# Modulation products of a decoder step on one Trainium2 core: 256 or 512 columns per product

## The chip, the core and the metric

The kernel runs on one core of a Trainium2 chip. The metric is device time in microseconds (us) of one execution; the median of three runs of the kernel before is 2639.03 us (2635.15 to 2641.7). In the profile PE is TensorE's matmul stream, PEld its weight loads, DVE is VectorE, ACT is ScalarE, POOL is GpSimd and SP is SyncE, which issues nearly all DMAs.

## The reference

One step of a decoder layer for 256 prompt tokens and 8 x 4 sample tokens (288 in all), width 4096, all in fp32. The part that matters here is the modulation of the normalised input, and of the output, by a projection of nine condition vectors (one prompt, eight samples):

```
m = jax.nn.silu(c) @ w_ada + b_ada                 # c: 9 x 4096, w_ada: 4096 x 12288
shift, scale, gate = jnp.split(m[:, None, :], 3, axis=-1)
h = _rmsnorm(x, g_norm) * (1 + scale) + shift
... = _split_in(h @ w_in)                          # w_in: 4096 x 14960, feeds three token mixers
x = x + gate * (mix @ w_out)                       # w_out: 4096 x 4096
```

The three mixers (a chunked gating MLP, a gated delta rule, a sparse attention with cached keys) lie between and are not touched.

## The kernel before

A planner in the kernel (class `Weaver`) holds a list of units and writes out every engine's instructions, running a model of the engines' times as it goes. A `Gemm` unit (kind "g") multiplies one 128-row k-tile of `w_in` or `w_out` by `h`: the raw weight tile is split by ACT and DVE into a high and a low part (`wh`, `wl`), and PE does three products for each of four 128-column tiles (`acc<-hH,wh`, `hL,wh`, `hH,wl`, 288 columns each). Raw tiles hold two k-tiles (512 KB) and rotate through `N_RAW` = 4 buffers `w`; splits run up to `N_SPLIT` = 4 units ahead of PE.

An `Ada` unit (kind "a") is a piece of `silu(c) @ w_ada`. Its stationary operand is 32 columns of `cT`, its moving operand a weight tile, and four products go to the four column quadrants of the array (`tile_position=(0, 32 * q)`), each into its own 32 partitions of one PSUM bank `ada`. Before, a unit loads one 512 KB tile and each quadrant takes 256 columns. Shift and scale are made in 11 sets, the first six of two k-tiles of `h` each and then five of four (`STEPS`, `ada_first`, tiles `wa`, `N_ADA` = 4 buffers), and gate in 4 sets (`ada_gate`, which uses the four `w` buffers). A set adds up over all of `w_ada`'s rows: 16 or 32 units. When it is complete, ACT copies the bank to SBUF, PE transposes it (`ada<-ident,adasb`), DVE adds the bias (`ada_raw`, `ada_fin1`, `ada_fin2`), and for shift and scale `make_h` makes the next rows of `h`.

Two stages follow each other. In the first (to about 812 us) the units of the next sets are spread between `Gemm` units of 45 column tiles per step; `LEAD` says how many units beyond a set's end are to be done when its step begins. In the second stage a gate unit follows every `GATE` = 4 `Gemm` units until all 128 are done (about 825 to 2062 us); the mixers' work is woven in between. Then come the output projection's units alone.

The list is kept in order on every queue: `prefetch` loads units strictly one after another as buffers come free (a unit whose buffer is taken holds up the loads of all units behind it), and SP issues the DMAs in that order. PE executes `Ada` units where they stand in the list.

Of the kernel before, what the change touches and what calls it, by code (L numbers as in the profile page):

```python
# [19 lines left out]
P = 128  # L20
# [29 lines left out]
GPAIR = 1  # L50
PLAN = {"p1": ["zc0", "zc1", "zb0", "zb1", "zb2", "zb3"], "attn": ["za0", "za1"], "dn3": []}
# [36 lines left out]
class Weaver:  # L88
# [214 lines left out]
    def prefetch(self, cur):  # L303

        u = self.units
        go = True
        while go:
            go = False
            if self.split < self.loaded:
                x = u[self.split]  # L310
                if x.kind == "a":
                    self.split += 1
                    go = True
                elif self.n_split < N_SPLIT and (self.at(x.raw.w) <= self.t["T"] + 0.5 or
                                                 not any(y.kind == "g" for y in u[cur + 1:self.split])):
# [20 lines left out]
    def run(self):  # L336
        self.prefetch(-1)
        for i, x in enumerate(self.units):
            for f in x.pre:
                f()  # L340
            self.finish(x.need)
            while self.split <= i:
                self.prefetch(i - 1)
            for n in range(x.steps):
                x.mm(n)
                if n == x.steps - 1:
                    if x.kind == "a":
                        self.release(x.tag, self.t["T"])
                    else:
                        self.n_split -= 2 if x.with_ else 1  # L350
                self.prefetch(i if n == x.steps - 1 else i - 1)
                self.stages()
            for f in x.post:
                f()
        self.finish(list(self.gens))


class Unit:
    def __init__(self, kind, tag, steps):
        self.kind, self.tag, self.steps = kind, tag, steps  # L360
        self.pre, self.need, self.post = [], [], []
        self.loads = True


class Box:
# [9 lines left out]
def tile_hybrid_step(ctx: ExitStack, tc: tile.TileContext, I, O):  # L375
# [134 lines left out]
    class Ada(Unit):  # L510
# [5 lines left out]
        def __init__(self, st, segs, ks, nk, finish, tag):  # L516
            super().__init__("a", tag, 1)
            self.st, self.segs, self.ks, self.nk, self.finish = st, segs, ks, nk, finish

        def do_load(self):  # L520
            n = sum(s[1] for s in self.segs)
            if self.tag == "wa":
                self.w = tl("p1", [P, self.nk, n], "wa", N_ADA)
            else:
                self.w = W.tile(wpool, [P, self.nk, n], F32, "w", "w", N_RAW)
            rows = w_ada[self.ks * P:(self.ks + self.nk) * P]
            if len(self.segs) == 2:
                (c0, m), (c1, _) = self.segs
                for k in range(self.nk):
                    dma(self.w[:, k].rearrange("p (s c) -> p s c", s=2),  # L530
                        rows[k * P:(k + 1) * P].rearrange("p (s c) -> p s c", c=c1 - c0)[:, 0:2, c0:c0 + m])
            else:
                ((c0, m),) = self.segs
                dma(self.w, rows[:, c0:c0 + m].rearrange("(k p) c -> p k c", p=P))

        def mm(self, j):
            if self.ks == 0:
                W.take()
                self.st.ps = pr("ada")
            n = sum(s[1] for s in self.segs) * self.nk // 4  # L540
            for q in range(4):
                k, o = (q % 2, q // 2) if self.nk == 2 else (0, q)
                kk = self.ks + k
                T.matmul(self.st.ps[32 * q:32 * q + 32, 0:n], cT[:, 9 * kk:9 * kk + 32], self.w[:, k, o * n:(o + 1) * n],
                         start=self.ks == 0, stop=self.ks + self.nk == KT, tile_position=(0, 32 * q))
            if self.ks + self.nk == KT:
                W.push(self.finish, front=True)

    def ada_raw(st, n):
        sb = W.tile(tmp, [P, 256], F32, "adasb", "adasb", 1)  # L550
        A.copy(sb[:, 0:n], st.ps[:, 0:n])
        yield
        free()
        yield from bank()
        p2 = pr4("ada2")
        for c in range(n // P):
            T.transpose(p2[:, c], sb[:, c * P:(c + 1) * P], ident)
        st.p2 = p2
        yield

    def ada_fin1(st, k0, n):

        yield from ada_raw(st, 256)
        yield lambda: prep_gens[0].done
        for which in range(2):
            src = st.p2[:, 0:2].rearrange("p h (q r) -> p q h r", r=32)[:, 2 * which:2 * which + 2, :, 0:9]
            dst = mod[which][:, k0:k0 + n, :].rearrange("p (q h) r -> p q h r", h=2)
            b = bT[:, which * 32 + k0:which * 32 + k0 + n].rearrange("p (q h) -> p q h", h=2)
            if n == 2:
                V.tensor_tensor(dst[:, 0], src[:, 0], b[:, 0, :, None].to_broadcast([P, 2, 9]), op=OP.add)  # L570
                V.tensor_tensor(dst[:, 0], dst[:, 0], src[:, 1], op=OP.add)
            else:
                V.tensor_tensor(dst, src, b[:, :, :, None].to_broadcast([P, 2, 2, 9]), op=OP.add)
            if which == 1:
                dst = mod[which][:, k0:k0 + n, :]
# [5 lines left out]
        yield from make_h(k0, n)  # L581

    def ada_fin2(st, f):
        yield from ada_raw(st, 256)
        src = st.p2[:, 0:2].rearrange("p h (q r) -> p q h r", r=32)[:, :, :, 0:9]
        b = bT[:, 64 + 8 * f:64 + 8 * f + 8].rearrange("p (q h) -> p q h", h=2)
        dst = gtT[:, 8 * f:8 * f + 8, :].rearrange("p (q h) r -> p q h r", h=2)
        V.tensor_tensor(dst, src, b[:, :, :, None].to_broadcast([P, 4, 2, 9]), op=OP.add)
# [1876 lines left out]
```

## Time and profile before

| | |
|---|---|
| median of three runs | 2639.03 us |
| the profiled execution | 2654.27 us, span 2652.5 us, mean granted PE clock 0.986 |
| busy: PE / PEld / DVE / ACT / POOL | 97% / 86% / 61% / 40% / 19% |
| DMA over the span | 616.11 MB, 232 GB/s |

Times of the trace come from that one execution; us count from its first instruction. "acc", "ada", "wa" are tile names; all instructions have line L71, since a recording layer issues them. One `ada` product shows as two records on PE, each with its weight load, so "x8" in a row of the timeline is one unit of four products. A record's length includes the time until its result is out, so what a run of instructions takes from PE is read from the starts of the instructions around it.

### The profile page before, as it was taken

How to read it: one execution, taken by the hardware profiler on the slowest of the kernel's cores; microseconds unless marked ns; L12 is line 12 of the kernel's file. 1: busy time of each engine (PE TensorE's matmuls, PEld its weight loads, DVE VectorE, ACT ScalarE, POOL GpSimd, SP SyncE). 2: the span in 40 equal slices, each digit the busy share in tenths (PEclk: the TensorE clock that was granted, in tenths of full speed). 3: DMA queues.
4: the chain of work that ended last, by engine and by line, in shares of the span. 5: the costliest groups of instructions: out<-in, count | busy, mean ns of one | idle time of the engine just before them, and what ended most of it. 6: DMA issues, size and time to landing. Idle time of an engine off the chain costs nothing.

```text
span 2652.5 us, 55324 instructions
## 1 busy us (share of the span) xinstructions
PE 2560.9 (97%) x21190; PEld 2279.1 (86%) x21190; DVE 1623.5 (61%) x3611; ACT 1062.0 (40%) x2440; POOL 492.3 (19%) x1137
## 2 busy tenths in 40 slices
PE   6999999999999999999999999999999999999997
PEld 3788888888888888877789989989989989999997
DVE  3477665555568786744467576567566567555554
ACT  3423222222245343333344444444443544444443
POOL 2000000000001042153543333343340210000000
PEclk9999999999999999999999999999999999999998
DMA  8999998998757576686776676577568565555565
GB/s 289 345 320 321 342 315 296 304 312 307 232 153 217 178 238 217 200 283 221 266 233 192 182 242 207 177 241 233 179 195 261 149 202 181 178 182 175 177 186 164
DMA packets 376032, 616.11 MB, mean 232 GB/s; under 512 B 48840, under 2 KB 149436, under 8 KB 375768
## 3 DMA queue, kind: packets, MB, share of 16 engines
q1 hardware_dynamic: 364728, 574.66, 67.8%
q0 software_dynamic: 11040, 37.92, 4.3%
q8 instruction: 167, 2.74, 0.4%
q14 instruction: 97, 0.79, 0.1%
HBM read 587.54 MB, written 24.95 MB: 231 GB/s over the span
## 4 chain that ended last, share of the span: by engine, by line
PE 86%; DMA 6%; DVE 2%; issue 2%; POOL 2%; ACT 1%; SPq 0%; another core or an unknown queue 0%; ACTq 0%; POOLq 0%; DVEq 0%
PE acc L71 68%; PE ada L71 7%; DMA wa<-in_w_ada_dram 2%; PE kT L71 1%; PE Sup L71 1%; DMA kraw<-in_cache_k_dram,ixk 1%; DVE wl L71 1%; PE YP L71 1%; DMA w<-in_w_in_dram 1%; PE v L71 1%; PE gram L71 1%; DMA vraw<-in_cache_v_dram,ixv 1%; PE o L71 1%; POOL vraw L71 1%; PE S L71 0%
## 5 line engine op out<-in xcount | busy, mean ns | idle before, releaser
L71 DVE TENSOR_TENSOR wl<-w,wh 128x512 fp32r<-128x512 f32 (+1 forms) x1216 | 806.1, 682 | 735.3 <-ACT wh L71 667.8
L71 ACT CAST wh<-w 128x512 fp32r<-128x512 f32 (+1 forms) x1216 | 717.3, 611 | 1232.3 <-PE acc L71 905.6
L71 PE MATMUL acc<-hH,wh 128*128 128x288 f32 (+1 forms) x3744 | 1180.2, 315 | 14.5 <-ACT hH L71 7.4
L71 PE MATMUL acc<-hL,wh 128*128 128x288 f32 (+1 forms) x3744 | 1110.4, 297 | 0.6 <-DVE hL L71 0.4
L71 PE MATMUL acc<-hH,wl 128*128 128x288 f32 (+1 forms) x3744 | 1108.4, 296 | 2.6 <-DVE wl L71 1.8
L71 PEld LDWEIGHTS acc<-hH,wh 128*128 128x128 f32 (+1 forms) x3744 | 708.4, 189 | 152.0 <-issue 81.9
L71 PEld LDWEIGHTS acc<-hL,wh 128*128 128x128 f32 (+1 forms) x3744 | 710.1, 190 | 6.7 <-issue 5.5
L71 PEld LDWEIGHTS acc<-hH,wl 128*128 128x128 f32 (+1 forms) x3744 | 709.1, 189 | 4.0 <-DVE wl L71 3.6
L71 PE MATMUL acc<-mL,wh 128*128 128x288 f32 x1024 | 302.6, 295 | 2.6 <-DVE mL L71 2.6
L71 PE MATMUL acc<-mH,wh 128*128 128x288 f32 x1024 | 304.4, 297 | 0.0
L71 PE MATMUL acc<-mH,wl 128*128 128x288 f32 x1024 | 302.7, 296 | 0.0
L71 PEld LDWEIGHTS acc<-mL,wh 128*128 128x128 f32 x1024 | 193.0, 189 | 2.9 <-DVE mL L71 2.9
L71 PEld LDWEIGHTS acc<-mH,wh 128*128 128x128 f32 x1024 | 193.0, 188 | 0.2
L71 PEld LDWEIGHTS acc<-mH,wl 128*128 128x128 f32 x1024 | 193.0, 188 | 0.0
L71 PE MATMUL ada<-wa,cT 128*32 128x256 f32 x2048 | 159.2, 395 | 15.8 <-DMA wa<-in_w_ada_dram 14.3
L71 PEld LDWEIGHTS ada<-wa,cT 128*32 128x32 f32 x2048 | 50.2, 109 | 66.9 <-issue 39.8
L71 DVE TENSOR_TENSOR zb<-zb,acc 128x288 f32<-128x288 f32 x160 | 70.9, 452 | 47.0 <-PE acc L71 45.7
L71 POOL TENSOR_TENSOR htmp<-yT,gaT 128x32 f32<-128x32 f32 x20 | 7.7, 382 | 460.0 <-DVE gaT L71 460.0
L71 PE MATMUL ada<-w,cT 128*32 128x256 f32 x1024 | 83.9, 393 | 1.9 <-issue 1.0
L71 POOL TENSOR_SCALAR frs<-frs 128x1 f32<-128x1 f32 (+1 forms) x3 | 0.9, 298 | 451.5 <-DVE frs L71 451.3
L71 DVE TENSOR_TENSOR R<-R,R 128x248 f32<-128x248 f32 (+30 forms) x248 | 72.6, 293 | 7.1 <-DMA R<-dD 0.5
L71 POOL TENSOR_SCALAR tap<-xp,cwT 128x32 f32<-128x32 f32 x144 | 75.8, 527 | 0.3
(457 smaller groups left out, 2387.0 us busy)
## 6 DMA issues: line engine op xcount, KB each, us to landing
w<-in_w_in_dram SPq DMA_DIRECT2D x464, 512.0 KB
wa<-in_w_ada_dram SPq DMA_DIRECT2D x160, 512.0 KB
w<-in_w_ada_dram SPq DMA_DIRECT2D x128, 512.0 KB
w<-in_w_out_dram SPq DMA_DIRECT2D x128, 512.0 KB
wa<-in_w_ada_dram SPq DMA_DIRECT2D x192, 256.0 KB
St<-in_state_dn_dram SPq DMA_DIRECT2D x16, 512.0 KB
out_dram<-St SPq DMA_DIRECT2D x16, 512.0 KB
X<-in_x_prompt_dram SPq DMA_DIRECT2D x8, 512.0 KB
```

The lines of the kernel that those rows point to most:

```text
L71: r = f(*a, **k)
```

## The change

A unit now takes two weight tiles (`n_load` = 2, `do_load` runs twice and appends to `w`). Each quadrant multiplies 512 columns: quadrants 0 and 1 take the two halves of the first tile, 2 and 3 those of the second. For shift and scale sets of two k-tiles the four quadrants are four different k-tiles; for the others each pair of quadrants is one k-tile. So there are half as many units of twice the width, and at the end of a set the quadrants hold partial sums that DVE adds. Per set the copy is 512 columns wide instead of 256 (from a tag `u2k` of two buffers that the conv stage's `prev` and `tailo` use too), and there are four transposes instead of two. `LEAD` goes from 10 to 5 and `GATE` from 4 to 8 units, the same number of tiles. Bytes, number and size of the DMAs stay.

```
-LEAD = 10
+LEAD = 5
-GATE = 4
+GATE = 8
...
                     x.do_load()
-                    self.loaded += 1
+                    x.n_load -= 1
+                    if not x.n_load:
+                        self.loaded += 1
...
                     if x.kind == "a":
-                        self.release(x.tag, self.t["T"])
+                        for _ in x.w:
+                            self.release(x.tag, self.t["T"])
...
         def mm(self, j):
...
-            n = sum(s[1] for s in self.segs) * self.nk // 4
             for q in range(4):
-                k, o = (q % 2, q // 2) if self.nk == 2 else (0, q)
-                kk = self.ks + k
-                T.matmul(self.st.ps[32 * q:32 * q + 32, 0:n], cT[:, 9 * kk:9 * kk + 32], self.w[:, k, o * n:(o + 1) * n],
+                kk = self.ks + q * self.nk // 4
+                w = self.w[q // 2].rearrange("p k n -> p (k n)")[:, q % 2 * 512:q % 2 * 512 + 512]
+                T.matmul(self.st.ps[32 * q:32 * q + 32], cT[:, 9 * kk:9 * kk + 32], w,
                          start=self.ks == 0, stop=self.ks + self.nk == KT, tile_position=(0, 32 * q))
...
-    def ada_raw(st, n):
-        sb = W.tile(tmp, [P, 256], F32, "adasb", "adasb", 1)
-        A.copy(sb[:, 0:n], st.ps[:, 0:n])
+    def ada_raw(st):
+        sb = W.tile(tmp, [P, 512], F32, "u2k", "adasb", 2)
+        A.copy(sb, st.ps)
...
-        for c in range(n // P):
+        for c in range(4):
             T.transpose(p2[:, c], sb[:, c * P:(c + 1) * P], ident)
...
             if n == 2:
-                V.tensor_tensor(dst[:, 0], src[:, 0], b[:, 0, :, None].to_broadcast([P, 2, 9]), op=OP.add)
-                V.tensor_tensor(dst[:, 0], dst[:, 0], src[:, 1], op=OP.add)
+                V.tensor_reduce(dst, st.p2[:, :, 2 * which:2 * which + 2].rearrange("p q c r -> p c r q"),
+                                axis=AX.X, op=OP.add)
+                V.tensor_tensor(dst, dst, b, op=OP.add)
             else:
-                V.tensor_tensor(dst, src, b[:, :, :, None].to_broadcast([P, 2, 2, 9]), op=OP.add)
+                V.tensor_tensor(dst, st.p2[:, which], b, op=OP.add)
+                V.tensor_tensor(dst, dst, st.p2[:, 2 + which], op=OP.add)
...
-        nk = 4 // n
+        nk = 8 // n
...
-        return [Ada(st, [(2 * D + f * 1024, 1024)], k, 1, fin, "w") for k in range(KT)]
+        return [Ada(st, [(2 * D + f * 1024, 1024)], k, 2, fin, "w") for k in range(0, KT, 2)]
```

Where the units stand is the planner's to say, so the order of the instructions is shown at three places. First PE, in the first step of the first stage, between two column tiles of `acc`; before:

```order
L71 MATMUL acc_1400<-hH_530,wh 128x288
L71 MATMUL acc_1400<-hL_542,wh 128x288
L71 MATMUL acc_1400<-hH_530,wl 128x288
L71 MATMUL ada<-wa,cT 32x256 x4
L71 MATMUL acc_1417<-hH_530,wh 128x288
L71 MATMUL acc_1417<-hL_542,wh 128x288
```

and now:

```order
L71 MATMUL acc_1413<-hH_500,wh 128x288
L71 MATMUL acc_1413<-hL_512,wh 128x288
L71 MATMUL acc_1413<-hH_500,wl 128x288
L71 MATMUL ada<-wa,cT 32x512 x4
L71 MATMUL acc_1447<-hH_500,wh 128x288
L71 MATMUL acc_1447<-hL_512,wh 128x288
```

"x4" is one unit, with 256 and with 512 columns. Before, PE's order has 102 such single units in the first stage and 75 runs of two or more in a row (256 units in 177 runs); now 128 units stand in 125 runs. Behind the first `acc` product the runs go from 166 to 119: from 72 to 60 in the six steps of two k-tiles, and from 94 to 59 after them. In the second stage, where every gate unit stands alone, they go from 128 to 64.

Second, SP's queue in the second stage, where `w<-in_w_ada_dram` is a gate tile and `w<-in_w_in_dram` a raw tile of a `Gemm` pair; before:

```order
L71 DMA w<-in_w_in_dram 128x2x512
L71 DMA mixD_185<-pz 128x256
L71 DMA w<-in_w_in_dram 128x2x512
L71 DMA w<-in_w_ada_dram 128x1024
L71 DMA w<-in_w_in_dram 128x2x512 x2
L71 DMA w<-in_w_ada_dram 128x1024
```

and now:

```order
L71 DMA prev<-in_state_conv_dram 24x512
L71 DMA w<-in_w_in_dram 128x2x512 x4
L71 DMA w<-in_w_ada_dram 128x1024 x2
L71 DMA w<-in_w_in_dram 128x2x512 x4
L71 DMA w<-in_w_ada_dram 128x1024 x2
```

Two raw tiles and one gate tile by turns became four raw tiles and two gate tiles, which share the same four buffers.

Third, DVE at the end of a shift and scale set of four k-tiles (`shT`, `gaT` are the shift and the scale, `zc` a running sum of the step); before:

```order
L71 TENSOR_TENSOR zc_918<-zc_918,acc_4138 128x288
L71 TENSOR_TENSOR shT<-ada_4119,bT 128x36
L71 TENSOR_TENSOR gaT<-ada_4119,bT 128x36
L71 SCALAR_TENSOR_TENSOR gaT<-gaT,gnT 128x36
L71 TENSOR_TENSOR zc_935<-zc_935,acc_4149 128x288
```

and now:

```order
L71 TENSOR_TENSOR zc_879<-zc_879,acc_3897 128x288
L71 TENSOR_TENSOR shT<-ada_3876,bT 128x36
L71 TENSOR_TENSOR shT<-shT,ada_3876 128x36
L71 TENSOR_TENSOR gaT<-ada_3876,bT 128x36
L71 TENSOR_TENSOR gaT<-gaT,ada_3876 128x36
L71 SCALAR_TENSOR_TENSOR gaT<-gaT,gnT 128x36
```

Each of the two rows of the modulation got one more add, of the other pair of quadrants.

## Rows read from the trace of the kernel before

**Rows 1.** The page, part 4: the chain that ended last, by engine.
```profile
PE 86%; DMA 6%; DVE 2%; issue 2%; POOL 2%; ACT 1%; SPq 0%; another core or an unknown queue 0%; ACTq 0%; POOLq 0%; DVEq 0%
```

**Rows 2.** Windows: us, busy PE, PEld, DVE, ACT, POOL, PEclk, DMA share, GB/s.
```profile
55.00:358.00 303.00, 300.07 (x2600) 245.60 (x2600) 191.15 (x420) 103.38 (x207) 14.64 (x48) 0.99 0.97 322
358.00:735.00 377.00, 371.89 (x3116) 311.93 (x3112) 205.20 (x409) 109.94 (x203) 10.87 (x32) 1.00 0.87 292
812.00:1050.00 238.00, 220.90 (x2123) 190.21 (x2122) 179.84 (x471) 100.00 (x256) 53.35 (x114) 0.96 0.67 209
1050.00:1500.00 450.00, 434.84 (x3622) 377.13 (x3622) 259.15 (x554) 183.87 (x468) 184.98 (x373) 0.98 0.71 228
1500.00:2060.00 560.00, 557.68 (x4610) 503.95 (x4609) 375.46 (x956) 251.48 (x695) 186.00 (x471) 1.00 0.70 215
```

**Rows 3.** Timeline of PE, one unit alone: start us, us, instruction.
```profile
265.79 0.29 PE L71 MATMUL acc<-hH,wl 128*128 128x288 f32 x1
266.01 0.64 PE L71 MATMUL ada<-wa,cT 128*32 128x256 f32 x8
266.58 0.40 PE L71 MATMUL acc<-hH,wh 128*128 128x288 f32 x1
266.82 0.29 PE L71 MATMUL acc<-hL,wh 128*128 128x288 f32 x1
266.95 0.29 PE L71 MATMUL acc<-hH,wl 128*128 128x288 f32 x1
```

**Rows 4.** Timeline of PE, two modulation units in a row.
```profile
118.67 0.29 PE L71 MATMUL acc<-hH,wl 128*128 128x288 f32 x1
118.89 1.07 PE L71 MATMUL ada<-wa,cT 128*32 128x256 f32 x16
119.89 0.40 PE L71 MATMUL acc<-hH,wh 128*128 128x288 f32 x1
120.13 0.29 PE L71 MATMUL acc<-hL,wh 128*128 128x288 f32 x1
```

**Rows 5.** Timeline of PE, one gate unit in the second stage.
```profile
1506.34 0.29 PE L71 MATMUL acc<-hH,wl 128*128 128x288 f32 x1
1506.57 0.64 PE L71 MATMUL ada<-w,cT 128*32 128x256 f32 x8
1507.13 0.40 PE L71 MATMUL acc<-hH,wh 128*128 128x288 f32 x1
1507.37 0.29 PE L71 MATMUL acc<-hL,wh 128*128 128x288 f32 x1
```

**Rows 6.** Tiles ada and Sup: duration ns min/median/max, first and last start, forms.
```profile
L71 PE MATMUL ada<-wa,cT x2048: 379/379/637, 20.1 to 730.4; 128*32 128x256 f32 x187
L71 PE MATMUL Sup<-R,R x64: 590/592/697, 1521.7 to 2165.4; 128*128 128x512 f32 x64
```

**Rows 7.** Timeline of PE, the transposes that end a modulation set.
```profile
1171.81 0.30 PE L71 MATMUL acc<-hH,wl 128*128 128x288 f32 x1
1171.94 0.38 PE L71 MATMUL ada<-ident,adasb 128*128 128x128 f32 x2
...
1172.29 0.29 PE L71 MATMUL acc<-hL,wh 128*128 128x288 f32 x1
```

**Rows 8.** Tile ada, and groups of ACT by shape: copies of two widths.
```profile
L71 ACT COPY adasb<-ada x15: 363/373/434, 50.3 to 2065.2; 128x256 f32<-128x256 f32 x15
L71 ACT COPY ktk<-kT 128x512 f32<-128x512 f32 x32 | 18.8, 588 | 28.3 <-PE kT L71 11.5 <-issue 8.5 <-ACT S L71 8.2
```

**Rows 9.** Waits of PE, PEld (55 to 741 us), ACT (812 to 2180).
```profile
PE acc L71 <- ACT hH L71: 7.4, 2, 4.0
PE ada L71 <- DMA wa<-in_w_ada_dram: 2.0, 2, 1.5
PEld ada L71 <- DMA wa<-in_w_ada_dram: 7.4, 15, 2.0
ACT wh L71 <- DMA w<-in_w_in_dram: 84.5, 36, 4.1
```

More of the change, by code (lines that the diff above doesn't have):

```diff
@@ L361, in __init__ @@
         self.pre, self.need, self.post = [], [], []
-        self.loads = True
+        self.loads, self.n_load = True, 1
 class Box:
@@ L518, in __init__ @@
             self.st, self.segs, self.ks, self.nk, self.finish = st, segs, ks, nk, finish
+            self.n_load, self.w = 2, []
         def do_load(self):
             n = sum(s[1] for s in self.segs)
+            nk = self.nk // 2
             if self.tag == "wa":
-                self.w = tl("p1", [P, self.nk, n], "wa", N_ADA)
+                w = tl("p1", [P, nk, n], "wa", N_ADA)
             else:
-                self.w = W.tile(wpool, [P, self.nk, n], F32, "w", "w", N_RAW)
-            rows = w_ada[self.ks * P:(self.ks + self.nk) * P]
+                w = W.tile(wpool, [P, nk, n], F32, "w", "w", N_RAW)
+            ks = self.ks + nk * len(self.w)
+            rows = w_ada[ks * P:(ks + nk) * P]
             if len(self.segs) == 2:
                 (c0, m), (c1, _) = self.segs
-                for k in range(self.nk):
-                    dma(self.w[:, k].rearrange("p (s c) -> p s c", s=2),
+                for k in range(nk):
+                    dma(w[:, k].rearrange("p (s c) -> p s c", s=2),
                         rows[k * P:(k + 1) * P].rearrange("p (s c) -> p s c", c=c1 - c0)[:, 0:2, c0:c0 + m])
@@ L533, in do_load @@
                 ((c0, m),) = self.segs
-                dma(self.w, rows[:, c0:c0 + m].rearrange("(k p) c -> p k c", p=P))
+                dma(w, rows[:, c0:c0 + m].rearrange("(k p) c -> p k c", p=P))
+            self.w.append(w)
         def mm(self, j):
@@ L555, in ada_raw @@
         p2 = pr4("ada2")
-        for c in range(n // P):
+        for c in range(4):
             T.transpose(p2[:, c], sb[:, c * P:(c + 1) * P], ident)
-        st.p2 = p2
+        st.p2 = p2.rearrange("p c (q r) -> p q c r", r=32)[:, :, :, 0:9]
         yield
     def ada_fin1(st, k0, n):
-        yield from ada_raw(st, 256)
+        yield from ada_raw(st)
         yield lambda: prep_gens[0].done
         for which in range(2):
-            src = st.p2[:, 0:2].rearrange("p h (q r) -> p q h r", r=32)[:, 2 * which:2 * which + 2, :, 0:9]
-            dst = mod[which][:, k0:k0 + n, :].rearrange("p (q h) r -> p q h r", h=2)
-            b = bT[:, which * 32 + k0:which * 32 + k0 + n].rearrange("p (q h) -> p q h", h=2)
+            dst = mod[which][:, k0:k0 + n, :]
+            b = bT[:, which * 32 + k0:which * 32 + k0 + n][:, :, None].to_broadcast([P, n, 9])
             if n == 2:
-                V.tensor_tensor(dst[:, 0], src[:, 0], b[:, 0, :, None].to_broadcast([P, 2, 9]), op=OP.add)
-                V.tensor_tensor(dst[:, 0], dst[:, 0], src[:, 1], op=OP.add)
-            else:
-                V.tensor_tensor(dst, src, b[:, :, :, None].to_broadcast([P, 2, 2, 9]), op=OP.add)
+                V.tensor_reduce(dst, st.p2[:, :, 2 * which:2 * which + 2].rearrange("p q c r -> p c r q"),
+                                axis=AX.X, op=OP.add)
+                V.tensor_tensor(dst, dst, b, op=OP.add)
+            else:
+                V.tensor_tensor(dst, st.p2[:, which], b, op=OP.add)
+                V.tensor_tensor(dst, dst, st.p2[:, 2 + which], op=OP.add)
             if which == 1:
-                dst = mod[which][:, k0:k0 + n, :]
                 g = gnT[:, k0:k0 + n]
@@ L583, in ada_fin2 @@
     def ada_fin2(st, f):
[L584 to L588, printed above, removed]
+        yield from ada_raw(st)
+        for o in range(2):
+            dst = gtT[:, 8 * f + 4 * o:8 * f + 4 * o + 4, :]
+            b = bT[:, 64 + 8 * f + 4 * o:64 + 8 * f + 4 * o + 4]
+            V.tensor_tensor(dst, st.p2[:, o], b[:, :, None].to_broadcast([P, 4, 9]), op=OP.add)
+            V.tensor_tensor(dst, dst, st.p2[:, 2 + o], op=OP.add)
         yield
```

## The prediction

> **What bounds the kernel now.** The chain that ended last comes first: PE holds 86% of it and DMA 6% [rows 1], so what PE spends is what the kernel spends, unless something stands in the way. Then the windows by stage, for where this is so: PE is busy for 300.1 of 303 us from 55 to 358 us, 371.9 of 377 from 358 to 735, 557.7 of 560 from 1500 to 2060; only from 812 to 1500 is it idle, for 17.1 + 15.2 = 32.3 us, where the mixers' chains hold it up [rows 2]. The same rows show who would be next: the DMA share is 0.97 at 322 GB/s in the first of these stretches and 0.87 in the second, 0.67 to 0.71 later [rows 2].
>
> A busy PE is not a PE that streams, so the timeline comes next, and there the starts, not the lengths. In a plain stream `acc` products start 0.13 us apart [rows 3]. Around one `ada` unit that stands alone, the last product before it and the second one behind it start 1.03 us apart; two plain intervals would be 0.26, so the unit takes 0.77 us from PE [rows 3]. Two units in a row span 1.46 us, so they take 1.20 [rows 4]. The second unit of a run thus costs 0.43 us, and the first 0.77: 0.43 us are the columns' streaming, and 0.34 us are paid once for each run, for going over to the quadrants and back. A gate unit of the second stage has the same 1.03 us [rows 5], so the price holds there.
>
> **The change part by part.** Streaming first. A half product with 256 columns lasts 379 ns, one with 512 columns over the whole array 592 ns [rows 6]: 213 ns for 256 columns more, 0.43 us for both halves of a product, which is just what a second unit costs. So the four quadrants run beside each other, and a 512-column unit should cost 0.34 + 2 x 0.43 = 1.20 us, as much as two units in a row did. No trace shows 512 columns on quadrants; if the quadrants no longer overlapped fully, streaming could at worst double (0.85 us for each of 192 units, 164 us), and less than the columns' time isn't to be had. I take the 0.43 of rows 4, the nearest.
>
> What is saved is therefore only the 0.34 us of each run that goes. Where units already stood in pairs, nothing is saved. The order counts 166 runs behind the first `acc` product of the first stage, and 119 now: 47 x 0.34 = 16.0 us. In the second stage all 128 gate units stood alone, and 64 do now: 64 x 0.34 = 21.8 us. Together 37.8 us, all of it on PE's path.
>
> Added at the end of each of the 15 sets: two transposes more. Two of them in a stream take 1172.29 - 1171.81 - 0.26 = 0.22 us [rows 7], so 15 x 0.22 = 3.3 us on PE. ACT's copy grows from 373 to 588 ns [rows 8] and DVE adds the parts; both lie beside a full PE except at the first and the last set, where PE stands until `h` is written (7.4 us in two waits [rows 9]). There 0.22 us for the copy, 0.22 for the transposes and 0.2 for DVE come on top; a reduce over a set's parts has no row, and I bound it by nothing and by the 0.59 us of the widest copy, which reads more than it does. Twice 0.6 makes 1.2 us. The shared `u2k` buffers cost nothing as long as few sets end among the conv rows; there are four such sets, and a wait there would delay a gate that the output stage alone uses.
>
> The added wait: a unit needs two landed tiles instead of one. Behind it on PE stand all `acc` products, and behind these the splits that wait for their buffers. On SP two loads now wait together for one unit's end, with the raw tiles of `Gemm` units behind them. The four buffers hold two units instead of four, but when PE comes to a unit the same four tiles are loaded or under way. Bounds: before, waits for modulation tiles were 2.0 us of PE and 7.4 us of PEld from 55 to 741 us [rows 9], so at best waiting once for two tiles where two units waited gives back 9.4 us; at worst each of 119 units waits for one more tile, 512 KB at 322 GB/s or 1.6 us, 190 us in all. In the same term stands the gain of the first stretch: with 12 runs fewer it would end 4.1 us earlier, and its bytes would need 326 GB/s where 322 took a share of 0.97 [rows 2]. I take 3 us lost, near the 9.4 us row and far from the 190, since lookahead in tiles is kept.
>
> The gate units hold two of the four `w` buffers instead of one. The cover is the splits' lead of four units (48 products of 0.13 us, 6.2 us): ACT waited for raw tiles 36 times, 84.5 us, 4.1 us at the longest [rows 9], and this lead hid it. If it went, each of 64 units could cost one transfer, 512 KB at 215 GB/s or 2.4 us, 156 us in all; a gain there I exclude, since what is hidden already can't be saved. I take nothing, by the 4.1 us that stayed under 6.2. Last, the 32.3 idle us from 812 to 1500 us are set by other engines' chains. Some 688/1248 of the 64 saved runs, 35 or 12 us, lie there; between nothing and 12 us of it is lost, and I take a quarter, 3 us, since PE is 95% busy there [rows 2].
>
> Sum: -16.0 - 21.8 + 3.3 + 1.2 + 3 + 3 = -27.3 us. The profiled execution took 2654.27 us, its span 2652.5; it lies 0.6% above the median of the three runs. So the span should become about 2625 us, and 2639.03 x (1 - 27.3/2654.27) = 2612 us is the time I predict.
>
> **A rule against this reading.** Rows 3 and 4 put the fixed cost on the run, not on the product, since eight products in a row pay it once. The Trainium skill says otherwise (TensorEngine Tiling (Array Packing), Instruction Overhead): each matmul carries an overhead of its own of about 60 cycles. By that figure, 768 products fewer would save 768 x 60 cycles at 2.4 GHz, 19 us, an estimate from that page. The trace disagrees: a second unit of four products costs its streaming alone, 0.43 us [rows 4].
>
> **The rivals.**
>
> A. The fixed cost belongs to each product. Then a lone unit's 0.34 us is 0.085 us for each of its four products, and 768 products fewer save 65 us: 2639 - 65 + 8 = 2582 us with the added work and losses. Against it: a pair would have taken 1.54 us, and took 1.20 [rows 3, 4]. The rule of the page above would act here in this way.
>
> B. DMA sets the first stage. Its 16.0 us turn into waits for tiles, as the share of 0.97 suggests; against it the 0.87 of the longer stretch [rows 2]. Left: -21.8 + 3.3 + 1.2 + 3 = -14.3 us, or 2625 us.
>
> C. Slower: the pair of tiles. PE reaches units whose first tile has landed and whose second has not, in the stretch where DMA is full, and waits 1.6 us for each. From 17 units on (27.3/1.6) the gain is gone; with 40 of the 119 it is 64 - 27 = +37 us, 2676 us. For it: 15 PEld waits and 2 PE waits for such tiles already [rows 9]; against it, only 9.4 us in all.
>
> D. The change does less than it says: the planner's new order, which differs on every engine, gives back what the runs save, through new waits in the mixers' chains (32.3 us idle before [rows 2]). Within 8 us of before, 2635 us.
>
> E. 512 columns on quadrants don't overlap: up to 164 - 27 = +137 us, 2776 us. Against it rows 4 and 6, where two units in a row ran at full rate.
>
> **How the numbers follow.** The forecast has 0.61 (its own range 2600 to 2622), B 0.16, A 0.03, D 0.10, C 0.08, E 0.02. About 0.3% (8 us) is what a measurement of this kernel can tell from no change; the bound for faster is 2631 us. Forecast, B and A are faster, 0.80; D is the 0.10 for the same, C and E the 0.10 for slower. The range goes from 2597 us (no loss at all is 2606, and the waits given back 2597) to 2634 us, which takes in B and most of D; outside are A, C and E and the ends of D.
>
> **What would show it.** Right: each 512-column unit takes about 1.20 us by the starts around it; PE's `ada` runs are 119 in the first stage behind the first `acc` and 64 in the second, with as many `acc` products; half records of `ada` last near 592 ns; the first stage ends some 12 us earlier and the gate units some 30 us earlier; waits for `wa` tiles stay near 9 us. Wrong: units of 1.6 us or more (E), waits of PE for `wa` of tens of us with the DMA share at 0.97 (B, C), more idle PE from 812 to 1500 us (D), a unit of 0.9 us (A).

## The result, and the profile after

The changed kernel takes 2654.52 us (median of four, 2652.17 to 2654.96), before took 2637.67 us beside it: a ratio of 1.0059 [1.0044, 1.0074], 17 us **slower** where 27 us faster was forecast. On two later occasions the ratio was 1.0049 both times. The kernel before itself had medians of 2637.7, 2649.7, 2642.5, 2646.8, 2640.8 and 2649.0 us on six occasions, on several chips, so below every kernel is given as a ratio to before of its own occasion, and its interval in brackets. The profiled executions hide the loss: before's took 2654.27 us, long for it, and the changed kernel's 2652.17 us. So the traces show what changed, and only the timed ratios show what it cost.

The chain still belongs to PE, with less of it than in [rows 1]:

```profile
PE 84%; DMA 7%; DVE 3%; POOL 2%; issue 1%; ACT 1%; SPq 0%; ACTq 0%; POOLq 0%; DVEq 0%
```

The windows of [rows 2], now:

```profile
55.00:358.00 303.00, 297.02 (x2096) 229.33 (x2100) 189.58 (x413) 103.83 (x203) 14.18 (x54) 0.99 0.96 319
358.00:735.00 377.00, 368.89 (x2689) 304.39 (x2681) 209.16 (x427) 112.64 (x208) 11.26 (x32) 1.00 0.87 296
812.00:1050.00 238.00, 218.98 (x2069) 189.86 (x2068) 181.74 (x475) 99.98 (x255) 54.37 (x115) 0.97 0.65 211
1050.00:1500.00 450.00, 431.74 (x3499) 378.01 (x3497) 264.68 (x560) 185.13 (x455) 188.23 (x379) 0.99 0.72 235
1500.00:2060.00 560.00, 547.16 (x4316) 493.63 (x4313) 372.67 (x960) 254.38 (x720) 187.44 (x469) 0.99 0.68 210
```

PE is less busy in every one of them: 3 us in each of the first two, 2 to 3 in the next two, 10.5 in the last. In these windows 21.6 us of what was saved on PE stand as idle time.

The price of a unit is what was predicted. One alone, as in [rows 3]: start us, us, instruction.

```profile
264.93 0.29 PE L71 MATMUL acc<-hH,wl 128*128 128x288 f32 x1
265.16 1.07 PE L71 MATMUL ada<-wa,cT 128*32 128x512 f32 x8
266.15 0.39 PE L71 MATMUL acc<-hH,wh 128*112 128x288 f32 x1
266.38 0.30 PE L71 MATMUL acc<-hL,wh 128*112 128x288 f32 x1
```

From 264.93 to 266.38 it is 1.45 us, less two plain intervals of 0.13, so 1.19 us for four products of 512 columns. (The median from start to start is 1.458 us over 116 such units of the first stage, and 1.457 over 44 gate units.) Durations of the products and of the copy (ns min/median/max, first and last start), answering to [rows 6, 8]:

```profile
L71 PE MATMUL ada<-wa,cT x1024: 592/616/1063, 19.1 to 728.4; 128*32 128x512 f32 x171
L71 PE MATMUL ada<-w,cT x512: 592/593/618, 835.1 to 2055.1; 128*32 128x512 f32 x171
L71 ACT COPY adasb<-ada x15: 585/587/609, 51.9 to 2059.8; 128x512 f32<-128x512 f32 x15
```

The waits of [rows 9] (us in total, times, longest), four from 55 to 741 us and ACT's from 812 to 2180:

```profile
PE ada L71 <- DMA wa<-in_w_ada_dram: 1.9, 4, 0.7
PEld ada L71 <- DMA wa<-in_w_ada_dram: 9.8, 16, 1.5
PE acc L71 <- ACT hH L71: 8.5, 2, 4.5
PE acc L71 <- DVE v_c L71: 3.9, 6, 1.1
...
ACT wh L71 <- DMA w<-in_w_in_dram: 107.7, 61, 4.3
```

The last row points to the raw tiles: ACT, which splits them, waits for them 61 times instead of 36, 107.7 us instead of 84.5. PE's order of the second stage is the same in five traces of the changed kernel's (itself, a0, g0, e1, g1) and in four of before's (itself, e0, e2, g2). The counts keep apart, 55 to 62 and 34 to 43; the sums nearly touch, 98.1 to 117.3 us and 78.0 to 96.3.

And there is one hole. At the end of the third q group the planner must finish the first gated-delta group (`end_prev`), and it is late. The same hole of 40 to 44 us stands in all five traces of this order, and in no other run below. The windows from 1530 to 1570 us, of before first and of the changed kernel second:

```profile
1530.00:1570.00 40.00, 39.25 (x289) 33.89 (x288) 24.64 (x66) 16.56 (x52) 11.99 (x32) 1.00 0.84 258
```

```profile
1530.00:1570.00 40.00, 27.58 (x222) 17.36 (x221) 20.73 (x79) 15.71 (x69) 17.33 (x49) 0.87 0.31 87
```

Besides the 12.4 us of idle time, the granted clock is 0.87 there instead of 1.00: behind the first idle time, 2.79 us, it stood for a while at the lower of its two levels (1.2 GHz instead of 2.4). Between two `acc` products PE has nothing but products of the delta rule, here cut to the edges and some waits (in brackets the idle time before, and who ended it):

```profile
1530.95 0.29 PE L71 MATMUL acc<-hH,wl 128*128 128x288 f32 x1
1534.04 0.33 PE L71 MATMUL kbT<-ident,R 128*128 128x128 f32 x1 [2.79 <-ACT R L71]
...
1548.01 0.33 PE L71 MATMUL oTs<-ident,R 128*128 128x128 f32 x1 [2.75 <-DVE R L71]
...
1564.89 1.10 PE L71 MATMUL Sup<-R,R 128*128 128x512 f32 x2 [1.31 <-DVE St L71]
1567.13 0.44 PE L71 MATMUL kbT<-ident,R 128*128 128x128 f32 x2 [1.15 <-ACT R L71]
...
1570.80 0.38 PE L71 MATMUL acc<-hH,wh 128*128 128x288 f32 x1
```

For the experiments, times between counts of `acc` products in the traces (0, first, 1620th and 4320th, which ends the first stage; the 7764th, which ends the third q group; the 10160th, about the last gate unit; PE's last instruction), in us:

| kernel | ratio to before | 0-1 | -1620 | -4320 | -7764 | -10160 | -end |
|---|---|---|---|---|---|---|---|
| before, again (e0) | 0.9995 | 49.8 | 301.8 | 455.6 | 754.1 | 445.7 | 618.5 |
| changed | 1.0059 | 51.8 | 305.2 | 448.2 | 761.2 | 437.8 | 621.9 |
| e1 gates only | 0.9995 | 49.0 | 300.8 | 452.4 | 761.0 | 436.9 | 620.4 |
| e2 first stage only | 1.0000 | 53.8 | 302.8 | 448.1 | 751.2 | 445.1 | 621.6 |
| e3 a gate unit per 4 | 1.0120 | 51.4 | 306.9 | 449.1 | 820.1 | 409.0 | 619.9 |
| a1 gates 2 units later | 1.0008 | 52.4 | 306.8 | 448.7 | 741.8 | 447.3 | 621.4 |
| b3 half the bytes, stage 1 | 0.9905 | 45.1 | 293.7 | 444.7 | 748.1 | 447.5 | 618.0 |
| b2 gates of 128 columns | 0.9948 | 53.9 | 306.2 | 445.3 | 739.0 | 437.7 | 616.4 |
| g3 gates, one tile | 0.9897 | 52.2 | 306.9 | 446.4 | 732.3 | 438.6 | 619.9 |
| h2 gate loads apart | 0.9936 | 52.5 | 305.8 | 448.4 | 740.2 | 437.6 | 623.6 |

Columns start at PE's first instruction. From the 4320th to the 7764th product the changed kernel's trace takes 4 to 7 us more than those of before and e0, and behind it 8 less. One and the same order scatters: in this stretch the changed kernel's took 758 to 768 us in five traces, before's 743.9 to 756.7 in four, and a1 took 741.8 where b1, the same gates behind before's first stage, took 753.3. So a difference of some 10 us in one row says little.

### The profile page after: what moved, and what is told of

It reads as the page before. It is cut to its first block, busy times and chain, and to the rows that moved or that the text cites. A ratio compares the mean times of both kernels' runs of the same rounds, so it can differ in the third digit from the quotient of the medians.

```text
span 2650.5 us, 52359 instructions
## 1 busy us (share of the span) xinstructions
PE 2539.2 (96%) x19684; PEld 2241.3 (85%) x19684; DVE 1629.8 (61%) x3633; ACT 1064.7 (40%) x2440; POOL 493.6 (19%) x1137
## 4 chain that ended last, share of the span: by engine, by line
PE 84%; DMA 7%; DVE 3%; POOL 2%; issue 1%; ACT 1%; SPq 0%; ACTq 0%; POOLq 0%; DVEq 0%
PE acc L71 66%; PE ada L71 7%; DMA w<-in_w_in_dram 2%; DMA kraw<-in_cache_k_dram,ixk 2%; DMA wa<-in_w_ada_dram 1%; PE Sup L71 1%; PE kT L71 1%; DVE wl L71 1%; DMA vraw<-in_cache_v_dram,ixv 1%; PE YP L71 1%; PE v L71 1%; PE o L71 1%; PE gram L71 1%; PE S L71 1%; POOL vraw L71 1%
## 5 line engine op out<-in xcount | busy, mean ns | idle before, releaser
L71 PE MATMUL acc<-hH,wh 128*128 128x288 f32 (+1 forms) x3744 | 1160.2, 310 | 15.0 <-ACT hH L71 8.5
L71 PE MATMUL ada<-wa,cT 128*32 128x512 f32 x1024 | 157.4, 611 | 14.1 <-DMA wa<-in_w_ada_dram 14.1
L71 POOL DMA_INDIRECT vraw<-in_cache_v_dram,ixv x64 | 66.8, 1043 | 33.6 <-PE so L71 12.4
L71 DVE SCALAR_TENSOR_TENSOR cv<-xp,cwT,cv 128x256 f32<-128x256 f32 x144 | 70.2, 487 | 3.6
```

The source lines that it names most:

```text
L71: r = f(*a, **k)
```

## The experiments

**First set: which half, and the deadline theory.** The theory: PE's saving in the second stage only brings PE earlier to the deadline at the 7764th product, where it waits for the late delta group. Rivals: the first stage's DMA, or the `w` buffers that a gate unit holds.

e0 is before once more.

> A second copy of the kernel before, so that a profiled execution of it stands beside timed ones of the same chip. Both theories below expect a ratio of 1.000 to the kernel before. If the profiled execution of before (2654.27 us, 15 us above its timed runs) was one long execution, the new one lies at 2637 to 2643 us and shows where the 15 us were; if profiling itself costs 15 us, it lies at about 2654 again.

0.9995 [0.9984, 1.0005]; its profiled execution took 2652.21 us among timed ones of 2644 to 2653. So profiling shows no cost of its own; this occasion was a long one, and why the first profiled execution of before was long stays open.

e1 and e2 make each half of the change alone (e1 narrow in the first stage, with `LEAD = 10`; e2 narrow in the gates, with `GATE = 4`), by a flag in `Ada`, with before's code for the narrow form:

```diff
...
-            self.n_load, self.w = 2, []
+            self.wide = WIDE1 if tag == "wa" else WIDE2
+            self.n_load, self.w = 1 + self.wide, []
...
```

> Only the gate sets take 512 columns (a unit after every 8 Gemm units); the first stage stands as before. Deadline theory (the saved PE time of the second stage is lost because the sample attention and the first delta group are finished late, uncovered, before the third q group ends): the second stage has the order of the changed kernel, so the loss is all here, +15 to +24 us against before, 2652 to 2662 us. Rival, the loss comes from the first stage (full DMA, units of two tiles): the gates' 21.8 us show, 2615 to 2622 us.

> Only the first stage's sets take 512 columns; the gate units stay at 256 columns after every 4 Gemm units, so the second stage has the order of the kernel before. Deadline theory: between -1 and -8 us against before (what the first stage gained by the traces), 2629 to 2637 us. Rival, the first stage lost time to DMA and pairs of tiles: +10 to +20 us, 2648 to 2658 us.

e1: 0.9995 [0.9983, 1.0006]; e2: 1.0000 [0.9988, 1.0012]. The gates' 21.8 us are not there, and the first stage's 16 us are not either. Neither half alone explains 0.5%: the deadline theory is wrong in size, and so is the rival. The hole is in e1's trace too (40.6 us without an `acc` product), and e1 is no slower than before, so the hole by itself doesn't make the 0.5%.

e3 fills the hole with gate units:

```diff
-GATE = 8
+GATE = 4
```

> The changed kernel with one edit, a gate unit after every 4 Gemm units instead of 8. Work, bytes and products are the same; 28 gate units more (28 x 1.2 = 34 us of PE) stand ahead of the end of the third q group. Deadline theory: they cover the stretch of about 40 us without an acc product, so 25 to 35 us less than the changed kernel, 2620 to 2630 us. Rival, the gate units' hold on the w buffers or their two loads at once cost the time: denser units are no better or worse, 2650 to 2675 us. Rival, PE is the bound throughout and the loss is elsewhere: the same as the changed kernel, 2650 to 2658 us.

1.0120 [1.0096, 1.0144], some 30 us slower than before and not the 25 to 35 us faster than the changed kernel that the theory asked for; on before's time in the result (2637.67 us) the ratio makes 2669 us, inside the 2650 to 2675 of the rival with the `w` buffers. The hole is gone, but the stretch up to the 7764th product takes 820 us, 59 more than the changed kernel's; some 34 of them are the gate units moved there, and the next stretch takes 29 less. ACT's waits from 812 to 2060 us:

```profile
ACT wh L71 <- DMA w<-in_w_in_dram: 194.9, 63, 9.9
```

Where gate tiles come twice as often, the raw tiles come later. This was no expectation of the deadline theory and outweighs it, and it is what that rival says.

**Second set: the order's phase.** a0 is the changed kernel again; a1 has `GATE0 = 2`; a2 `BACKLOG = 3.0`; a3 `GPAIR = 2`, one edited line each.

> A second copy of the changed kernel, beside runs of before on the same chip. If the 0.6% of the result holds from chip to chip, the ratio is 1.004 to 1.008. If the two halves of the change add up as they did apart (gates alone 0.9995, first stage alone 1.000), it is 0.998 to 1.001, and the 2638 us of before in the result belong to other conditions than its profiled 2654 us.

> The changed kernel with the gate units 2 Gemm units later (GATE0 = 2, a unit after the 9th, 17th, ... Gemm unit instead of the 7th or 8th). Number, size and spacing of the gate units are the same. By the order on PE the first delta group's last products (oTs, Sup) now stand 60 column products ahead of the end of the third q group, not bunched at it. Deadline theory: the stretch of 40 us without an acc product goes, 15 to 25 us less than the changed kernel. Rival, the chain is late whatever the order and other waits take its place: within 6 us of the changed kernel. Rival, the two w buffers that a gate unit holds are the cost: within 6 us of the changed kernel, since they are held as often.

> The changed kernel with the planner's BACKLOG at 3.0 us instead of 2.0: chains are woven in while VectorE or ScalarE stand up to 3 us ahead of PE in its model. By the order the first delta group's end stands 200 column products ahead of the deadline, earlier than in the kernel before; gate units and their loads are unchanged. Deadline theory: 15 to 25 us less than the changed kernel. Rival, a chain that is placed earlier on PE only waits there for gathers, ACT and DVE: within 8 us of the changed kernel, and the waits of so, kT and osm for POOL, DMA and ACT grow by as much as the bunch at the deadline falls.

> The changed kernel with gate units two at a time, after every 16 Gemm units. By the order the first delta group's end stands 170 column products ahead of the deadline. Deadline theory alone: 15 to 25 us less than the changed kernel, and up to 11 us more, since 32 more switches (0.34 us each) go. Theory of the w buffers (a gate tile holds a buffer from its load until PE has used it): four gate tiles in a row take all four buffers, no raw tile can be loaded meanwhile, and each of 32 pairs costs PE 1 to 3 us, 30 to 100 us more than without; ACT's waits for raw tiles then grow from 44 us in 812 to 1500 us to over 150.

a0: 1.0049 [1.0031, 1.0067]. a1: 1.0008 [0.9997, 1.0019]. a2: 1.0014 [1.0004, 1.0023]. So without the hole 9 to 11 us come back, not 15 to 25: part turns into other waits, in a1 these of `prevT` (812 to 2060 us):

```profile
PE prevT L71 <- DMA prev<-in_state_conv_dram: 6.8, 6, 1.9
PEld prevT L71 <- DMA prev<-in_state_conv_dram: 5.8, 5, 2.1
```

Without the hole the kernel is within 0.14% of before, and no faster: the hole is not where its gain went. Nor does it have one price, since with the first stage as before the hole is there in e1 and costs nothing that shows.

a3: 1.0652 [1.0635, 1.0670], 160 us more than a0, 5 us for each of 32 pairs, in which four gate tiles take all four buffers; 30 to 100 were expected. PE itself now stands waiting for splits, and its granted clock is lower too (0.93 and 0.94 from 812 to 1500 and from 1500 to 2060 us, against 0.98 and 0.99 in the changed kernel), so not all of the 160 us is waiting:

```profile
ACT wh L71 <- DMA w<-in_w_in_dram: 174.9, 49, 15.4
PEld acc L71 <- ACT wh L71: 139.3, 28, 6.8
PE acc L71 <- ACT wh L71: 113.9, 28, 5.9
```

**Third set: what PE's time and DMA's bytes are worth.** b1 is e1 with `GATE0 = 2`, b4 before with it. b2 and b3 start from a1. b2 leaves out part of the gate's products, and its planner still counts them in full, so that the order stays; b3 leaves out half of the shift and scale weights:

```diff
 b2
...
+                c = 128 if self.tag == "w" and 0 < self.ks < KT - self.nk else 512
-                T.matmul(self.st.ps[32 * q:32 * q + 32], cT[:, 9 * kk:9 * kk + 32], w,
+                T.matmul(self.st.ps[32 * q:32 * q + 32, 0:c], cT[:, 9 * kk:9 * kk + 32], w[:, 0:c],
...
 b3
-            self.n_load, self.w = 2, []
+            self.n_load, self.w = 1 if tag == "wa" else 2, []
...
-                w = self.w[q // 2].rearrange("p k n -> p (k n)")[:, q % 2 * 512:q % 2 * 512 + 512]
+                w = self.w[q // 2 % len(self.w)].rearrange("p k n -> p (k n)")[:, q % 2 * 512:q % 2 * 512 + 512]
```

> Only the gate sets take 512 columns, and their units stand 2 Gemm units later (GATE0 = 2); the first stage is that of before. The second stage has the order of a1_gate0_2. Deadline theory: what a1_gate0_2 gained against the changed kernel (11 us) is gained here too, and the first stage's waits are not paid: ratio to before 0.994 to 0.998. Rival, the first stage with 512 columns is worth something after all: 1.000 to 1.004, slower than a1_gate0_2.

> a1_gate0_2 with 56 of the 64 gate units (all but the first and the last of each set) multiplying 128 columns on each quadrant instead of 512: part of the gate is left out. Loads, buffers, waits and the order of all instructions are the same, so PE alone has 56 x 3 x 0.21 = 36 us less to do between 825 and 2062 us (0.85 us for 512 columns, 0.21 for 128, from the price of a unit). Theory that PE's time is the bound there: 30 to 36 us less than a1_gate0_2, ratio to before 0.987 to 0.990. Rival, the mixers' chains and their deadlines set the pace: less than half of it comes out, 0.995 to 1.000, and the PE time saved stands as new waits of prevT, Sup, so and kT.

> a1_gate0_2 with the first stage's units loading one tile and using it for both pairs of quadrants: half of the shift and scale weights (67 MB) is left out. The products, the runs and the second stage's order are the same. Theory that DMA took the first stage's 16 us: from the first acc product to the 4320th it takes 12 to 20 us less than in a1_gate0_2 (755.5 us), besides an earlier first product (the first set's 16 MB become 8). Rival, 512-column units cost PE more in the first stage than the price of 1.20 us says, or the splits of raw tiles hold it: within 5 us of 755.5.

> The kernel before with its gate units 2 Gemm units later (GATE0 = 2, half a period): nothing else is changed. Deadline theory: the first delta group ends in time in either order (by the order 140 and 210 column products ahead of the deadline), so within 4 us of before, 0.9985 to 1.0015. Rival, any shift of the order moves the time by some 10 us, and a1_gate0_2's gain over the changed kernel is of that sort: a ratio beyond 0.997 or 1.003.

b1: 1.0001 [0.9992, 1.0011]; it missed its 0.994 to 0.998, so wide gates gain nothing in this phase either. b4: 0.9966 [0.9954, 0.9977]: the same shift makes the kernel before 9 us faster, where the deadline theory allowed 4. A shift of the order is worth some 10 us to either kernel, as the rival said, and the 9 to 11 us of a1 and a2 are no more than that.

b2: 0.9948 [0.9936, 0.9960], 0.6% or 16 us less than a1's ratio of an earlier occasion, for 36 us less of PE's work (a unit of 128 columns spans 0.818 us from start to start, one of 512 columns 1.457). Of a1's time in the trace 3 us go up to the 7764th product, 10 behind it, 5 in the end stage, which has no gate unit (with a scatter of 11 us in the first of these). So about half of PE's time, or less, comes out in the second stage.

b3: 0.9905 [0.9890, 0.9920]. From the first to the 4320th product it takes 738.4 us; a1 took 755.5, before (e0) 757.4, so the 12 to 20 us expected against a1 are there. With DMA out of the way (share of 0.76 and 0.65 in the windows of the first stage) the saving is there, and larger than predicted:

```profile
55.00:358.00 303.00, 301.30 (x2206) 237.93 (x2206) 202.13 (x434) 107.57 (x210) 13.50 (x48) 1.00 0.76 232
358.00:735.00 377.00, 369.50 (x2692) 311.78 (x2692) 211.28 (x425) 114.42 (x208) 11.19 (x32) 0.99 0.65 202
```

The edit changes two things at once: the bytes, and the `wa` buffers, of which a unit now holds one of four instead of two. No run holds the buffer without the bytes in this stage, so the two are not told apart here; the share of 0.96 in the changed kernel's first window speaks for the bytes.

**Fourth set: do the halves add up, and what does the second gate tile cost?** g0, g1 and g2 are the changed kernel, e1 and e2 again, on one occasion. g3 is the changed kernel with b3's edit for `tag == "w"` in place of `"wa"`.

> The changed kernel once more, beside its two halves and before on the same occasion, since before itself took 2637.7, 2649.7, 2642.5 and 2646.8 us on four occasions. Theory that the halves add up: its ratio is the product of the two ratios below within 0.002. Rival, they do not (the first stage's end shifts what the second stage meets): it is 0.003 or more away from that product. By the earlier ratios 1.0059 and 1.0049 it lies at 1.003 to 1.007.

> The gates alone at 512 columns, a second time (0.9995 the first time). If the changed kernel's loss is the second stage's order alone, 1.003 to 1.007 here; if the first measurement holds, 0.998 to 1.001.

> The first stage alone at 512 columns, a second time (1.000 the first time). Theory that DMA takes what PE saves there: 0.998 to 1.002. If the changed kernel's loss comes from here after all, 1.003 to 1.006.

> The changed kernel with a gate unit loading one tile and using it for both pairs of quadrants: half of the gate's weights (33.5 MB) is left out, PE's products are the same, and a unit holds one of the four w buffers as before. By the order on PE the first delta group's end then stands 180 column products ahead of the deadline, as in the kernel before. Theory that the second w buffer costs (raw tiles come later, so splits and chains come later): 13 to 26 us less than the changed kernel, ratio to before 0.993 to 0.999, and ACT's waits for raw tiles from 812 to 2060 us back from 98 to 108 us towards 84. Rival, the buffers cost nothing and only the order's phase is unlucky: since the phase changes here too, no more than a1_gate0_2 gained, 1.000 to 1.002.

g0: 1.0049 [1.0034, 1.0064]; g1: 1.0024 [1.0010, 1.0038]; g2: 1.0002 [0.9989, 1.0015]. The product of the halves is 1.0026; the difference of 0.0023 lies between the expectation (0.002) and its rival (0.003), and is about what the three intervals leave open. But the gates alone stand at 0.9995 and 1.0024 in two measurements, the first stage alone at 1.0000 and 1.0002, and both together at 1.0059, 1.0049 and 1.0049. Taken together, the halves leave 0.3 to 0.4% that neither shows alone, and no run shows where it stands. What is shown is that neither half gains.

g3, which leaves out half of the gate's weights: **0.9897** [0.9879, 0.9915], 39 us less than g0 and 25 less than before, beyond the 13 to 26 us and the 1.000 to 1.002 that were expected. With one tile to a unit the gates' 21.8 us are there. Its order has no hole either, so the 39 us are not the second tile's alone. ACT's waits for raw tiles from 812 to 2060 us, in g0 and then in g3:

```profile
ACT wh L71 <- DMA w<-in_w_in_dram: 117.3, 62, 4.1
```

```profile
ACT wh L71 <- DMA w<-in_w_in_dram: 4.9, 3, 2.8
```

**Fifth set: its buffer, its bytes or its place.** h1 loads 64 columns of the second tile, lets all quadrants use the first (so half of the gate is left out), and reads the second with one small product so that its buffer stays held. h2 takes the two loads apart by a load order of its own:

```diff
 h1
-                dma(w, rows[:, c0:c0 + m].rearrange("(k p) c -> p k c", p=P))
+                if self.w:
+                    m = 64
+                dma(w[:, :, 0:m], rows[:, c0:c0 + m].rearrange("(k p) c -> p k c", p=P))
...
 h2
+SHIFT = (0, 1)
...
+                    held += [[s, x] for s in SHIFT]
...
+            if x.kind == "g" and x.loads:
+                for h in held:
+                    h[0] -= 1
+            lo += [h[1] for h in held if h[0] <= 0]
...
-                x = u[self.loaded]
+                x = self.lo[self.loaded]
```

> The changed kernel whose gate units load the first tile whole and of the second only 64 of 1024 columns; both pairs of quadrants use the first tile, and one more product of 64 columns per unit reads the second, so that its w buffer is held as long as in the changed kernel. Most of the second tiles (31 MB) is left out. Theory of the hold (two of four w buffers out of use until PE has been at the unit): the raw tiles still come late, ACT's waits for them from 812 to 2060 us stay near 100 us, ratio to before 1.000 to 1.005. Rival, the bytes (a second 512 KB transfer ahead of the raw tiles): as with one tile, ACT's waits near 5 us, ratio 0.988 to 0.993. By the order on PE the first delta group ends 140 column products ahead of the deadline, so an unlucky end plays no part in it.

> The changed kernel with the second tile of a gate unit loaded one raw pair later than the first (tile, raw pair, tile instead of tile, tile, raw pair). Bytes, products and units are the same, and both buffers are still held. By the order on PE the first delta group ends 140 column products ahead of the deadline. Theory that the two transfers in a row are what keeps raw tiles back: ACT's waits for raw tiles fall below 60 us and the ratio to before is 0.990 to 0.996. Rival, the buffers held or the bytes as such: the waits stay near 100 us and the ratio is 0.999 to 1.003, as with a1_gate0_2.

h1: 0.9939 [0.9920, 0.9958]. h2: 0.9936 [0.9917, 0.9954], the whole computation, faster than either kernel by 0.6 and 1.1%. ACT's waits in h1 and in h2:

```profile
ACT wh L71 <- DMA w<-in_w_in_dram: 77.7, 49, 4.1
```

```profile
ACT wh L72 <- DMA w<-in_w_in_dram: 67.5, 37, 4.8
```

h2 hit its ratio, 0.990 to 0.996, and missed its waits, below 60 us. h1 lies between its theory and the rival in both. Against the changed kernel 1.1% comes back with the bytes gone, or moved behind a raw pair. But neither order has the hole, and a shift of the order was worth up to 0.4%. The fair comparison is with the orders without a hole that load both tiles in a row: a1 1.0008, a2 1.0014 and b1 1.0001. Against these h2 gains 0.7%, still more than any shift gave, so loading the tiles apart is worth something here, by this comparison 0.7%, with up to 0.4% of it open to the order. Against before, shifted to its better order (b4, 0.9966), h2 is 0.3% faster. The buffer held as such is no large cost: h1 takes 0.4% more than g3, and its extra product alone lengthens a unit from 1.457 to 1.568 us, 7 us or 0.27% for 64 units.

The waits are the weaker witness. ACT's scatter with one order of the gates (112.8, 105.0, 116.8 and 76.5 us in a1, b1, b2 and b3). PEld's waits for split tiles (`acc` for `wh`, 812 to 2060 us) grew from 1.2 us before to 19.6, but are 18.9 in g3 and 17.0 in h2, which gain. By which waits of PE the second tile costs its time is not shown. In h2 PE is full again where the changed kernel's was not (1500 to 2060 us; 12.4 of the changed kernel's 12.8 idle us there lie in the hole):

```profile
1500.00:2060.00 560.00, 558.27 (x4450) 508.38 (x4449) 383.32 (x977) 263.81 (x722) 184.66 (x467) 1.00 0.70 216
```

## Why the prediction was wrong

**The price of a unit: right.** 1.20 us predicted, 1.19 measured, in both stages; E falls with it, and A (0.9 us). By the Trainium skill (TensorEngine Tiling (Array Packing), Instruction Overhead) each product carries its own overhead; the trace disagrees a second time, since at these widths four wide products (1.458 us from start to start in the median) cost what eight narrow ones in a row did (1.462).

**First stage, -16.0 + 3 us: the saving was right, and the term for the waits mis-sized.** The changed trace takes 3.6 us less than before's from the first to the 4320th product, and e2 and g2 measure nothing in all. b3, with half of the bytes and buffers, takes 19 us less. So waits for tiles take 12 to 16 us, not 3. This was rival B's mechanism, given 0.16. The step that failed judged the stage by the 0.97 of its first part and the 0.87 of its second [rows 2] and by 9.4 us of waits for modulation tiles [rows 9], and these hardly grew. It left out the waits for raw tiles, which share the DMA: ACT's from 55 to 741 us, before first and the changed kernel second:

```profile
ACT wh L71 <- DMA w<-in_w_in_dram: 123.0, 41, 5.8
```

```profile
ACT wh L71 <- DMA w<-in_w_in_dram: 130.0, 45, 6.0
```

In b3 ACT has no such wait in this stretch. The row of before was there to be read; but it says only what DMA costs at the old pace. The estimate had even noted that the first stretch would need 326 GB/s; it got 319.

**Gates, -21.8 us with "I take nothing" for the `w` buffers: this step failed.** The argument was a cover of 6.2 us over a longest wait of 4.1 us [rows 9]. It compared one wait with the cover, and overlooked that before its unit had one 512 KB tile between raw tiles, and now two in a row. The longest wait hardly grew (4.3 us); the number of waits did, from 36 to 61. In place of nothing, the second tile in a row costs about as much as the gates save: the gates alone measure 0.9995 and 1.0024, and h2, with the same bytes, products and buffers but a raw pair between the two tiles, 0.9936. e3 and a3 show what happens when gate tiles come denser (+31 and +172 us against before), g3 what happens with one tile to a unit (the gain arrives). The 84.5 us should have been read the other way: a queue that already makes ACT wait 36 times has little slack for a second tile. That a3 lost about the bound of 156 us is chance, since its pairs and their waits are others.

**Chains, +3 us: too small, and in the wrong place.** Idle PE time was expected where it had been, between 812 and 1500 us; the largest came at a deadline that before met in time, 40 us in which PE is busy for 27.6. That is rival D's mechanism. Orders without the hole are 9 to 11 us faster (a1 and a2), but the same shift gains 9 us in before, which has no hole, and e1 has the hole and loses nothing; so its price by itself is not shown. In the sum of rival A the added work and losses are 10.5 us, not 8, which decides nothing.

**End of sets, +3.3 + 1.2 us: near.** 60 transposes stand for 30, the copy lasts 587 ns (588 predicted), the first `acc` product comes 2 us later (0.6 predicted; e2 and g0 2 to 4), perhaps because the last unit of the first set waits for two tiles; with one tile to a unit, and half of the bytes, it comes 7 us earlier (b3 against a1).

C was the right side for the wrong reason, which is luck: the waits of PE and PEld for modulation tiles hardly grew (9.4 us before [rows 9], 11.7 now); it was the raw tiles behind them that came late.

**What stays open:** where the 0.3 to 0.4% stand that only both halves together lose; how much of the 0.5% is the hole, since each edit also moves the order, and one order's stretch varied by 10 to 13 us between traces; by which of PE's waits the second gate tile costs its time; and whether bytes or held buffers take the first stage's gain.

## What to carry to other kernels

When a change makes one engine's work cheaper, ask first what feeds that stretch: here a DMA share of 0.97, and a queue for whose tiles ACT already waited in both stages, stood in the profile of before, and none of the 38 us that PE saved came out. A unit that needs two transfers should not issue them one behind the other in a queue that others live on: one raw pair between them turned 0.5% slower into 0.6% faster, of which up to 0.4% may be the shifted order. And where a planner re-orders everything, shift the order by a little in both kernels before believing 0.3%: it moved each by as much.

## What the runs showed of the hardware that was not expected

The same instructions in the same order on PE do not take the same time in the stretch with the gathers, from the 4320th to the 7764th product: 743.9 to 756.7 us in four traces of before's order, and 758 to 768 in five of the changed kernel's. The first stage of before's order is steadier, 300.2 to 302.3 and 452.4 to 455.6 us for its two parts in six traces. And the kernel before moved by 0.45% between occasions, almost as much as the effect that was to be measured, and by 0.27% between two occasions on one and the same chip.

Within an occasion, the length of a run goes with TensorE's granted clock. In 108 runs of before on five occasions, 0.001 less of mean granted clock goes with 1.6 to 2.4 us more (correlation -0.70 to -0.89). The changed kernel's median is 0.985 where before's is 0.988 to 0.989. At that rate this is 5 to 10 us of the 13 to 17 lost, an estimate from these runs. But a1, b1 and b2, which are no slower than before, stand at 0.984 to 0.986 as well, so whether the lower clock is part of the cause or only follows PE's idle time is not shown.
